# Moving the products of the forget and decay sums three slab pairs back, with their tables in a tile of their own

## The chip, the cores and the metric

The kernel runs on one core of a Trainium2 chip. The metric is the device time of one execution in microseconds (us); several executions are measured, and their median is given.

## What is computed

One layer of a decoder with two token mixers that read the same normalized input `h` (1024 tokens by 1024 channels): a state-space branch (SSD) and an attention branch with forget gates. Cut to what the change touches:

```python
proj = h @ w_in                       # slabs z, xbc, dt, q, k, v, z_att, f, gates
dt = softplus(dt_raw + dt_bias)       # 16 heads
a = dt * -exp(a_log)
a_cs = cumsum(a within chunks of 128 tokens)
lmat = exp(a_cs[l] - a_cs[s])         # decay inside a chunk; exp(a_cs) also carries the states
log_f = log_sigmoid(f_logit + b_f)    # 8 heads
f_cum = cumsum(log_f over all 1024 tokens)
logits = q k^T * scale + f_cum[q] - f_cum[k]
```

Both sums along tokens are made by matrix products: a lower triangle of ones sums within a block of 128 tokens, and a matrix of ones adds what lies in earlier blocks.

## The kernel before

The matrix products run in float32 as three products of a high and a low half (`hh` and `hl` for the input, `wh` and `wl` or `sh` and `sl` for the weights). The work has these stages: the normalized input and its halves; a first slab of v with the columns of `dt` and `f`; then 19 pairs of weight slabs of 128 columns (`PAIRS`, counted here from 0); then the SSD stage mixed with the rest of v and some of q and k; attention; and the output products.

A pair (`c_pair`, from line 463) is computed by a scheme with seven products instead of eight: VectorE makes sums and differences of the four raw weight tiles (lines 481 to 484), ScalarE rounds each of the seven forms to its high half and GpSimd makes the low half (`split`, lines 102 and 103), TensorE does seven products of 12 matmuls each over tiles of 128 by 512 (lines 499 to 501: high by high, high by low, low by high), and VectorE adds the products up in PSUM (lines 508 to 521). The forms are named `f1`, `f6`, `f7`, `f5`, `f4`, `f2`, `f3` in this order. The products go into eight PSUM buffers, three of the pool `mm` and five of the pool `pp`; a product can start only when its buffer's earlier product has been taken out.

What takes a product out depends on the slab. A gate slab has a tanh on ScalarE (line 188). A slab for the convolution is copied to `xp` (line 538), and when both halves are there VectorE makes four passes of 128 by 1024 and a last product (lines 542, 545 and 548, with a tanh on ScalarE between, line 547). A slab for z has a tanh on ScalarE (line 528) and a product on VectorE that reads the PSUM buffer (line 529, into `zt`). Pairs 0 and 2 are gates, pairs 1, 3 and 5 are convolutions, pair 4 is z. In front of some pairs the kernel also makes sums of the later stages' weights (`w_sums`, lines 583 to 598: loads, two sums on VectorE at 590 and 591, two on GpSimd, stores).

The softplus chain `dt_chain` (lines 366 to 402) is called in front of pair 2. It loads 24 columns for 1024 tokens from `d_scr` into the tile `tmp` (line 622), computes the softplus by a series on VectorE (lines 372 to 385, one exponential on ScalarE), negates the forget part into a table `lf` of 64 columns (line 390), makes the running sums over blocks `pre` in another 64 (line 394), and multiplies both by `tri` and `ones` on TensorE (lines 396 and 397). The result is copied (line 399) and stored to `f_scr` (line 400), which the attention stage reads. `tmp` is one of four buffers of the pool `ev` that also holds the slabs on their way out, so its tables last only as long as it is held. `ssm_sums` (lines 404 to 430), called in front of pair 3, does the same for the decay: `a` from `dt` (line 407), three products (412 to 414), and copies and exponentials into `acs`, `dec`, `ed`, `a_scr` and `e_scr`, which the SSD stage reads.

The order on each engine is not that of the code: a scheduler places the instructions ahead of time by an estimate, engine by engine, and on the chip each engine then executes its list strictly in order. A list's instruction that waits holds up all that stand behind it on the same engine. The DMAs are all issued by SyncE (SP), also in order.

Of the kernel before, what the change touches and what calls it, by code (L numbers as in the profile page):

```python
# [24 lines left out]
F32 = mybir.dt.float32  # L25
# [6 lines left out]
P = 128  # L32
# [37 lines left out]
def build(ctx, tc, t):  # L70
    nc = tc.nc
    V, A, G, PE, SP = nc.vector, nc.scalar, nc.gpsimd, nc.tensor, nc.sync

    const = ctx.enter_context(tc.tile_pool(name="const", bufs=1))
# [8 lines left out]
    def ev(name):  # L83
        return evp.tile([P, 1028], F32, tag="ev", bufs=4, name=name)
# [63 lines left out]
    ones = const.tile([P, P], F32, name="ones")  # L148
    V.memset(ones, 1.0)
    tri = const.tile([P, P], F32, name="tri")  # L150
# [9 lines left out]
    f_scr = dram.tile([64, P], F32, name="f_scr")  # L160
# [170 lines left out]
    dt = const.tile([P, NC, SH], F32, name="dt")  # L331
    acs = const.tile([P, NC, SH], F32, name="acs")
    dec = const.tile([P, NC, SH], F32, name="dec")
    ed = const.tile([P, NC, 8], F32, name="ed")

    def gate_slab(j):
        evac, store = gate_out(j)
        c_slab(t["w_c"], G0 + j, hh, hl, evac)
        store()
# [23 lines left out]
    with tc.tile_pool(name="pa", bufs=1, side="right") as pa, \  # L363
            tc.tile_pool(name="pap", bufs=1, space=PSUM) as pap:

        def dt_chain(dtf, tmp):

            def sl(i):
                return tmp[:, i * 192:(i + 1) * 192].rearrange("p (c n) -> p c n", n=24)
            b3 = hb[:, 0:24].rearrange("p (o n) -> p o n", o=1).broadcast_to([P, 8, 24])  # L370
            v, e, s, p = dtf, sl(1), sl(2), sl(3)
            V.tensor_tensor(out=v, in0=v, in1=b3, op=ALU.add)
            V.tensor_scalar(out=v[:, :, 16:24], in0=v[:, :, 16:24], scalar1=-1.0, scalar2=None, op0=ALU.mult)
            V.scalar_tensor_tensor(out=e, in0=v, scalar=-1.0, in1=v, op0=ALU.mult, op1=ALU.max)
            A.activation(out=e, in_=e, func=AF.Exp, scale=-1.0)
            V.tensor_scalar(out=s, in0=e, scalar1=2.0, scalar2=None, op0=ALU.add)
            V.reciprocal(out=s, in_=s)
            V.tensor_tensor(out=s, in0=s, in1=e, op=ALU.mult)
            V.tensor_tensor(out=e, in0=s, in1=s, op=ALU.mult)
            V.tensor_scalar(out=p, in0=e, scalar1=1.0 / 15, scalar2=None, op0=ALU.mult)  # L380
            for n in (13, 11, 9, 7, 5, 3):
                V.scalar_tensor_tensor(out=p, in0=p, scalar=1.0 / n, in1=e, op0=ALU.add, op1=ALU.mult)
            V.scalar_tensor_tensor(out=p, in0=p, scalar=1.0, in1=s, op0=ALU.add, op1=ALU.mult)
            V.tensor_scalar(out=v, in0=v, scalar1=0.0, scalar2=None, op0=ALU.max)
            V.scalar_tensor_tensor(out=v, in0=p, scalar=2.0, in1=v, op0=ALU.mult, op1=ALU.add)


            lf = tmp[:, 192:256].rearrange("p (h c) -> p h c", h=8)
            pre = tmp[:, 256:320].rearrange("p (h c) -> p h c", h=8)
            V.tensor_scalar(out=lf, in0=v[:, :, 16:24].rearrange("p c h -> p h c"), scalar1=-1.0, scalar2=None,  # L390
                            op0=ALU.mult)
            V.memset(pre[:, :, 0:1], 0.0)
            for c in range(1, 8):
                V.tensor_tensor(out=pre[:, :, c:c + 1], in0=pre[:, :, c - 1:c], in1=lf[:, :, c - 1:c], op=ALU.add)
            ps = pap.tile([P, 512], F32, tag="pp", bufs=5, name="pp")
            PE.matmul(ps[0:64, 0:P], lhsT=tmp[:, 192:256], rhs=tri, start=True, stop=False)
            PE.matmul(ps[0:64, 0:P], lhsT=tmp[:, 256:320], rhs=ones, start=False, stop=True)
            ft = tmp[0:64, 320:320 + P]
            V.tensor_copy(out=ft, in_=ps[0:64, 0:P])
            SP.dma_start(out=f_scr, in_=ft)  # L400

            V.tensor_copy(out=dt, in_=v[:, :, 0:16])

        def ssm_sums():
            a = ev("a")
# [205 lines left out]
        tmp = ev("tmp")  # L611
# [7 lines left out]
        for n, (sa, sb) in enumerate(PAIRS):  # L619
            if n == 2:  # L620
                tmp = ev("tmp")
                SP.dma_start(out=tmp[:, 0:192], in_=d_scr)
                dt_chain(tmp[:, 0:192].rearrange("p (c n) -> p c n", n=24), tmp)
            if n == 3:
                ssm_sums()
            for wn, p in WPREP.get(n, ()):
                if wn == "g":
                    gb = out_gate(gb, p)
                elif wn == "G":
                    gb = gate_sum(gb)  # L630
                else:
                    w_sums(wn, p, gb if wn == "o" else None)
            (ea, fa), (eb, fb) = slab_out(sa), slab_out(sb)
            c_pair(sa, sb, ea, eb)
            fa()
            fb()


    with tc.tile_pool(name="sd", bufs=1, side="right") as sd, \
# [152 lines left out]
        for tb in range(8):  # L792
            PE.matmul(rps[:, 2 * tb:2 * tb + 1], lhsT=sacc[:, tb * P:(tb + 1) * P], rhs=ones[:, 0:1],
                      start=True, stop=True)
        rc = const.tile([P, 8], F32, name="rc")
        V.tensor_scalar(out=rc, in0=rps[:, 0:16].rearrange("p (a two) -> p a two", two=2)[:, :, 0],
                        scalar1=1.0 / 1024, scalar2=4 * EPS, op0=ALU.mult, op1=ALU.add)
        G.tensor_tensor(out=rc, in0=rc, in1=mhalf, op=ALU.pow)
# [287 lines left out]
    with tc.tile_pool(name="finp", bufs=1, space=PSUM) as fpp_:  # L1086
# [73 lines left out]
        for i in OOUT:  # L1160
# [7 lines left out]
            if i != OOUT[-1]:  # L1168
                ps = [bank() for _ in range(4)]
# [6 lines left out]
            else:  # L1176
                fs = [w_in("o", i, k) for k in range(4)]
                for tb in range(4):
                    ps = bank()
# [70 lines left out]
```

## Time and profile before

| | us |
|---|---|
| median of 3 runs | 1305.86 |
| lowest and highest | 1300.53, 1307.06 |
| the profiled execution | 1302.24 |
| its span, first to last instruction | 1300.5 |
| TensorE busy | 1182.4 |
| VectorE busy | 934.5 |
| GpSimd busy | 759.7 |
| ScalarE busy | 594.6 |

The profile is of one execution. In a timeline each row has the start, the duration, the engine (PE is TensorE, DVE is VectorE, ACT is ScalarE, POOL is GpSimd, SP is SyncE), the line, the instruction with its output and inputs, how many were merged (x), and in brackets how long the engine had been idle and what it waited for. Matmuls overlap: a row of 0.39 us is followed by the next after 0.23. Lists of groups give the count, the busy time, the mean of one in ns, and the idle time before.

### The profile page before, as it was taken

How to read it: one execution, taken by the hardware profiler on the slowest of the kernel's cores; microseconds unless marked ns; L12 is line 12 of the kernel's file. 1: busy time of each engine (PE TensorE's matmuls, PEld its weight loads, DVE VectorE, ACT ScalarE, POOL GpSimd, SP SyncE). 2: the span in 40 equal slices, each digit the busy share in tenths (PEclk: the TensorE clock that was granted, in tenths of full speed). 3: DMA queues.
4: the chain of work that ended last, by engine and by line, in shares of the span. 5: the costliest groups of instructions: out<-in, count | busy, mean ns of one | idle time of the engine just before them, and what ended most of it. 6: DMA issues, size and time to landing. Idle time of an engine off the chain costs nothing. (4 is left out here: it accounts for less than half of the span.)

```text
span 1300.5 us, 18848 instructions
## 1 busy us (share of the span) xinstructions
PE 1182.4 (91%) x6206; PEld 988.6 (76%) x6206; DVE 934.5 (72%) x1610; ACT 594.6 (46%) x1194; POOL 759.7 (58%) x636
## 2 busy tenths in 40 slices
PE   4889929998998899999988999999999998999896
PEld 3678817876876688799878888888887786888685
DVE  6855474976799576546779873555566978999997
ACT  5453313323233233377667743445456453354354
POOL 3226543556666466627878876445446645687666
PEclk9899969999998899999999999999999999999998
DMA  8664541345438375655646648633227518666234
GB/s 343 236 220 137 181 148 63 127 153 175 173 85 301 121 256 186 226 196 157 213 153 186 192 155 294 224 112 99 91 99 232 189 66 304 219 197 196 56 114 145
DMA packets 109022, 228.29 MB, mean 176 GB/s; under 512 B 12362, under 2 KB 20220, under 8 KB 107900
## 3 DMA queue, kind: packets, MB, share of 16 engines
q1 hardware_dynamic: 108924, 227.09, 52.4%
q8 instruction: 49, 0.80, 0.2%
q14 instruction: 49, 0.40, 0.1%
HBM read 159.14 MB, written 67.90 MB: 175 GB/s over the span
## 5 line engine op out<-in xcount | busy, mean ns | idle before, releaser
L103 POOL TENSOR_TENSOR wl<-wr,wh 128x512 fp32r<-128x512 f32 (+1 forms) x188 | 280.2, 1502 | 166.6 <-ACT wh L102 149.8
L102 ACT CAST wh<-wr 128x512 fp32r<-128x512 f32 (+1 forms) x214 | 129.3, 618 | 177.8 <-DMA wr<-w_c 64.7
L103 POOL TENSOR_TENSOR sl<-sr,sh 128x512 fp32r<-128x512 f32 x57 | 91.1, 1605 | 87.4 <-ACT sh L102 74.6
L116 PE MATMUL mm<-hl,wh 128*128 128x512 f32 x288 | 116.8, 405 | 1.8 <-DVE hl L310 1.8
L115 PE MATMUL mm<-hh,wh 128*128 128x512 f32 x288 | 115.8, 407 | 0.4 <-DVE ql L972 0.4
L117 PE MATMUL mm<-hh,wl 128*128 128x512 f32 x288 | 116.1, 404 | 0.0
L140 PE MATMUL mm<-wh,hh 128*128 128x256 f32 (+1 forms) x256 | 74.3, 292 | 4.9 <-DVE tmp L351 4.9
L102 ACT CAST sh<-sr 128x512 fp32r<-128x512 f32 x57 | 33.8, 617 | 93.5 <-DVE sr L482 74.3
L141 PE MATMUL mm<-wl,hh 128*128 128x256 f32 (+1 forms) x256 | 74.5, 292 | 0.0
L142 PE MATMUL mm<-wh,hl 128*128 128x256 f32 (+1 forms) x256 | 74.4, 292 | 0.0
L1027 ACT ACTIVATE pr<-pr,sm 128x1024 f32<-128x1024 f32 (+3 forms) x64 | 49.9, 780 | 51.5 <-DVE sm L1026 42.1
L1030 POOL TENSOR_SCALAR pr<-pr,sm 128x1024 f32<-128x1024 f32 (+3 forms) x64 | 48.8, 765 | 36.0 <-DVE sm L1029 29.3
L1022 DVE CUSTOM_DVE_ANT_0 pr<-lg,fb 128x512 f32<-128x512 f32 (+1 forms) x96 | 51.6, 551 | 21.5 <-PE lg L1021 13.1
L116 PEld LDWEIGHTS mm<-hl,wh 128*128 128x128 f32 x288 | 55.4, 192 | 13.4 <-DVE hl L310 2.6
L117 PEld LDWEIGHTS mm<-hh,wl 128*128 128x128 f32 x288 | 55.3, 192 | 10.9
L1013 POOL TENSOR_SCALAR_AFFINE_SELECT fb<-fb 128x128 f32<-128x128 f32 x64 | 21.0, 330 | 71.9 <-DVE sm L1022 58.0
L1046 DVE TENSOR_TENSOR ptl<-tp,pth 128x512 fp32r<-128x512 f32 (+1 forms) x80 | 50.1, 632 | 17.9 <-ACT pth L1045 17.6
L115 PEld LDWEIGHTS mm<-hh,wh 128*128 128x128 f32 x288 | 54.8, 193 | 10.4 <-DVE ql L972 0.6
L1045 ACT CAST pth<-tp 128x512 fp32r<-128x512 f32 (+1 forms) x80 | 42.4, 543 | 40.5 <-PE tp L1042 31.3
L692 ACT ACTIVATE ab<-ab,acs 128x128 f32<-128x128 f32 x128 | 41.0, 391 | 32.2 <-DMA ab<-a_scr 30.5
L140 PEld LDWEIGHTS mm<-wh,hh 128*128 128x128 f32 x256 | 49.1, 193 | 5.3 <-DVE tmp L351 5.1
L141 PEld LDWEIGHTS mm<-wl,hh 128*128 128x128 f32 x256 | 49.4, 193 | 0.2
(401 smaller groups left out, 3923.5 us busy)
## 6 DMA issues: line engine op xcount, KB each, us to landing
wr<-w_c SPq DMA_DIRECT2D x116, 256.0 KB, 3.5
wa<-w_ada SPq DMA_DIRECT2D x8, 1024.0 KB, 11.3
g_scr<-gt SPq DMA_DIRECT2D x16, 512.0 KB, 4.1
ab<-a_scr SPq DMA_DIRECT2D x32, 256.0 KB, 3.6
gt<-g_scr SPq DMA_DIRECT2D x32, 256.0 KB, 3.2
wr<-w_ps SPq DMA_DIRECT2D x28, 256.0 KB, 2.9
wr<-w_pa SPq DMA_DIRECT2D x28, 256.0 KB, 3.1
wr<-so SPq DMA_DIRECT2D x28, 256.0 KB, 2.7
```

The lines of the kernel that those rows point to most:

```text
L102: A.copy(out=hi[:, :n], in_=raw[:, :n])
L103: eng.tensor_tensor(out=lo[:, :n], in0=raw[:, :n], in1=f32(hi[:, :n]), op=ALU.subtract)
L115: PE.matmul(ps, lhsT=hi[:, cs], rhs=xh[k][:, hs], start=(k == 0), stop=False)
L116: PE.matmul(ps, lhsT=hi[:, cs], rhs=xl[k][:, hs], start=False, stop=False)
L117: PE.matmul(ps, lhsT=lo[:, cs], rhs=xh[k][:, hs], start=False, stop=(k == 7))
L140: PE.matmul(o, lhsT=xh[k][:, ts], rhs=hi[:, cs], start=(k == 0), stop=False)
L141: PE.matmul(o, lhsT=xh[k][:, ts], rhs=lo[:, cs], start=False, stop=False)
L142: PE.matmul(o, lhsT=xl[k][:, ts], rhs=hi[:, cs], start=False, stop=(k == 7))
L1022: V.tensor_tensor_reduce(out=pr[:, n0:n1], in0=lg[:, :n1 - n0], in1=fb[:, n0:n1], op0=ALU.add, op1=ALU.min, scale=1.0, scalar=BIG, accum_o ...
L1027: A.activation(out=pr[:, :n], in_=pr[:, :n], func=AF.Exp, scale=-1.0, bias=sm[:, 0:1], accum_out=sm[:, 1:2])
L1030: G.tensor_scalar(out=pr[:, :n], in0=pr[:, :n], scalar1=sm[:, 1:2], scalar2=0.5, op0=ALU.mult, op1=ALU.mult)
L1046: V.tensor_tensor(out=ptl[:, :w], in0=tp[:, :w], in1=f32(pth[:, :w]), op=ALU.subtract)
```

## The change

`dt_chain` now writes `lf` and `pre` into a new constant tile `fl` (128 by 128), so that they last when `tmp` is given back, and ends with the copy to `dt`. The two products, the copy and the store of the forget sums become `f_sums`; the copy goes back into `fl`. `f_sums` and `ssm_sums` are both called in front of pair 5, instead of in front of pair 2 (inside the chain) and pair 3. At the end of the SSD stage the tile `rc` of 8 columns takes the first columns of `fl` instead of a tile of its own. Line numbers behind the new tile are one or two higher.

```diff
--- before.py
+++ after.py
@@ -332,6 +332,7 @@
     acs = const.tile([P, NC, SH], F32, name="acs")
     dec = const.tile([P, NC, SH], F32, name="dec")
     ed = const.tile([P, NC, 8], F32, name="ed")
+    fl = const.tile([P, P], F32, name="fl")
 
     def gate_slab(j):
         evac, store = gate_out(j)
@@ -385,21 +386,21 @@
             V.scalar_tensor_tensor(out=v, in0=p, scalar=2.0, in1=v, op0=ALU.mult, op1=ALU.add)
 
 
-            lf = tmp[:, 192:256].rearrange("p (h c) -> p h c", h=8)
-            pre = tmp[:, 256:320].rearrange("p (h c) -> p h c", h=8)
+            lf = fl[:, 0:64].rearrange("p (h c) -> p h c", h=8)
+            pre = fl[:, 64:128].rearrange("p (h c) -> p h c", h=8)
             V.tensor_scalar(out=lf, in0=v[:, :, 16:24].rearrange("p c h -> p h c"), scalar1=-1.0, scalar2=None,
                             op0=ALU.mult)
             V.memset(pre[:, :, 0:1], 0.0)
             for c in range(1, 8):
                 V.tensor_tensor(out=pre[:, :, c:c + 1], in0=pre[:, :, c - 1:c], in1=lf[:, :, c - 1:c], op=ALU.add)
+            V.tensor_copy(out=dt, in_=v[:, :, 0:16])
+
+        def f_sums():
             ps = pap.tile([P, 512], F32, tag="pp", bufs=5, name="pp")
-            PE.matmul(ps[0:64, 0:P], lhsT=tmp[:, 192:256], rhs=tri, start=True, stop=False)
-            PE.matmul(ps[0:64, 0:P], lhsT=tmp[:, 256:320], rhs=ones, start=False, stop=True)
-            ft = tmp[0:64, 320:320 + P]
-            V.tensor_copy(out=ft, in_=ps[0:64, 0:P])
-            SP.dma_start(out=f_scr, in_=ft)
-
-            V.tensor_copy(out=dt, in_=v[:, :, 0:16])
+            PE.matmul(ps[0:64, 0:P], lhsT=fl[:, 0:64], rhs=tri, start=True, stop=False)
+            PE.matmul(ps[0:64, 0:P], lhsT=fl[:, 64:128], rhs=ones, start=False, stop=True)
+            V.tensor_copy(out=fl[0:64], in_=ps[0:64, 0:P])
+            SP.dma_start(out=f_scr, in_=fl[0:64])
 
         def ssm_sums():
             a = ev("a")
@@ -621,7 +622,8 @@
                 tmp = ev("tmp")
                 SP.dma_start(out=tmp[:, 0:192], in_=d_scr)
                 dt_chain(tmp[:, 0:192].rearrange("p (c n) -> p c n", n=24), tmp)
-            if n == 3:
+            if n == 5:
+                f_sums()
                 ssm_sums()
             for wn, p in WPREP.get(n, ()):
                 if wn == "g":
@@ -792,7 +794,7 @@
         for tb in range(8):
             PE.matmul(rps[:, 2 * tb:2 * tb + 1], lhsT=sacc[:, tb * P:(tb + 1) * P], rhs=ones[:, 0:1],
                       start=True, stop=True)
-        rc = const.tile([P, 8], F32, name="rc")
+        rc = fl[:, 0:8]
         V.tensor_scalar(out=rc, in0=rps[:, 0:16].rearrange("p (a two) -> p a two", two=2)[:, :, 0],
                         scalar1=1.0 / 1024, scalar2=4 * EPS, op0=ALU.mult, op1=ALU.add)
         G.tensor_tensor(out=rc, in0=rc, in1=mhalf, op=ALU.pow)
```

On TensorE, in before, between the product of pair 2 with the form `f4` (into the buffer mm_1754) and the one with `f1` (into pp_1696); `tmp` and `tri` are the tables named above:

```order
L501 MATMUL mm_1754<-thb2_1204,wl_1681 128x512
L499 MATMUL mm_1754<-thb3_1228,wh_1680 128x512
L500 MATMUL mm_1754<-tlb3_1229,wh_1680 128x512
L501 MATMUL mm_1754<-thb3_1228,wl_1681 128x512
L396 MATMUL pp_1622<-tri_76,tmp_1593 64x128
L499 MATMUL pp_1696<-hh0_240,wh_1664 128x512
L500 MATMUL pp_1696<-hl0_248,wh_1664 128x512
L501 MATMUL pp_1696<-hh0_240,wl_1665 128x512
```

In the changed kernel, TensorE's list behind the same product with `f4` (now mm_1750) has the one with `f2` (pp_1765, on `hh4` to `hh7`); those with `f1` and `f6` have moved ahead of those with `f7`, `f5` and `f4`, and no product of the sums is in pair 2:

```order
L502 MATMUL mm_1750<-thb2_1205,wl_1677 128x512
L500 MATMUL mm_1750<-thb3_1229,wh_1676 128x512
L501 MATMUL mm_1750<-tlb3_1230,wh_1676 128x512
L502 MATMUL mm_1750<-thb3_1229,wl_1677 128x512
L500 MATMUL pp_1765<-hh4_244,wh_1680 128x512
L501 MATMUL pp_1765<-hl4_252,wh_1680 128x512
L502 MATMUL pp_1765<-hh4_244,wl_1681 128x512
L500 MATMUL pp_1765<-hh5_245,wh_1680 128x512
```

So the matmul of line 396 has left this place, and the order of the seven products within pair 2 is now that of the code.

On TensorE, in before, at the end of pair 4: the last matmuls of its product with `f3` (mm_2147), and behind them the first product of pair 5 (pp_2216, `f1`):

```order
L501 MATMUL mm_2147<-hh6_246,sl_2049 128x512
L499 MATMUL mm_2147<-hh7_247,sh_2048 128x512
L500 MATMUL mm_2147<-hl7_255,sh_2048 128x512
L501 MATMUL mm_2147<-hh7_247,sl_2049 128x512
L499 MATMUL pp_2216<-hh0_240,wh_2184 128x512
L500 MATMUL pp_2216<-hl0_248,wh_2184 128x512
L501 MATMUL pp_2216<-hh0_240,wl_2185 128x512
L499 MATMUL pp_2216<-hh1_241,wh_2184 128x512
```

The same place in the changed kernel: behind the product with `f3` (mm_2126) stand the two products of the forget sums (lines 400 and 401), and behind those pair 5's product with `f2` (mm_2290), which in before stood sixth in its pair:

```order
L500 MATMUL mm_2126<-hh7_247,sh_2027 128x512
L501 MATMUL mm_2126<-hl7_255,sh_2027 128x512
L502 MATMUL mm_2126<-hh7_247,sl_2028 128x512
L400 MATMUL pp_2144<-tri_76,fl_836 64x128
L401 MATMUL pp_2144<-ones_74,fl_836 64x128
L500 MATMUL mm_2290<-hh4_244,wh_2205 128x512
L501 MATMUL mm_2290<-hl4_252,wh_2205 128x512
L502 MATMUL mm_2290<-hh4_244,wl_2206 128x512
L500 MATMUL mm_2290<-hh5_245,wh_2205 128x512
```

The sums have come to this place, and the product into an `mm` buffer has moved ahead of `f1`; the decay sums' three products follow it.

On VectorE, in before, the end of pair 3's convolution (cv_1999), the weight sums (sr_2344) and pair 4's products for z (zt_2008, zt_2007; mm_2115 holds the product with `f4`):

```order
L548 SCALAR_TENSOR_TENSOR cv_1999<-xp_1839,cv_1999 128x1024
L591 TENSOR_TENSOR sr_2344<-sr_2343,wr_2335 128x512
L529 SCALAR_TENSOR_TENSOR zt_2008<-zt_2008,pp_2098 128x512
L518 TENSOR_TENSOR mm_2131<-mm_2131,pe_2052 128x512
L529 SCALAR_TENSOR_TENSOR zt_2008<-zt_2008,mm_2115 128x512
L521 TENSOR_TENSOR mm_2147<-mm_2147,pe_2055 128x512
L535 MEMSET xp_2165 128x3
L529 SCALAR_TENSOR_TENSOR zt_2007<-zt_2007,mm_2131 128x512
L529 SCALAR_TENSOR_TENSOR zt_2007<-zt_2007,mm_2147 128x512
```

The same place in the changed kernel (cv_1978, sr_2345, zt_1987, zt_1986; mm_2094 holds the product with `f4`):

```order
L549 SCALAR_TENSOR_TENSOR cv_1978<-xp_1818,cv_1978 128x1024
L592 TENSOR_TENSOR sr_2345<-sr_2344,wr_2336 128x512
L530 SCALAR_TENSOR_TENSOR zt_1987<-zt_1987,pp_2077 128x512
L519 TENSOR_TENSOR mm_2110<-mm_2110,pe_2031 128x512
L530 SCALAR_TENSOR_TENSOR zt_1987<-zt_1987,mm_2094 128x512
L522 TENSOR_TENSOR mm_2126<-mm_2126,pe_2034 128x512
L408 SCALAR_TENSOR_TENSOR a_2149<-dt_832,hb_81 128x128
L402 COPY fl_836<-pp_2144 64x128
L530 SCALAR_TENSOR_TENSOR zt_1986<-zt_1986,mm_2110 128x512
L530 SCALAR_TENSOR_TENSOR zt_1986<-zt_1986,mm_2126 128x512
```

The start of the decay sums (a_2149) and the copy of the forget sums (fl_836) now stand between pair 4's products for z, behind the one that reads mm_2094.

## The prediction

> **What bounds the kernel now.** I read the page first, slice by slice, to see which engine is full in the stage that is edited; then the list of waits of TensorE, then its timeline around the longest wait, then VectorE's timeline in the same stretch, since VectorE is named as releaser. On the page the share of each engine comes first, then the 40 slices of 32.5 us:
>
> ```profile
> PE 1182.4 (91%) x6206; PEld 988.6 (76%) x6206; DVE 934.5 (72%) x1610; ACT 594.6 (46%) x1194; POOL 759.7 (58%) x636
> PE   4889929998998899999988999999999998999896
> PEclk9899969999998899999999999999999999999998
> ```
>
> TensorE is busy for 91% of the span and is the bound nearly everywhere; only slice 6 (162 to 195 us) is nearly empty, and the granted clock falls there too. The waits of TensorE between 120 and 320 us, and its timeline on both sides of the longest (start, duration, instruction, idle time before it):
>
> ```profile
> PE pp L396 <- DVE tmp L390: 26.3, 1, 26.3
> ...
> 162.35 0.39 PE L499 MATMUL mm<-tha,wh 128*128 128x512 f32 x1
> ...
> 170.42 0.40 PE L501 MATMUL mm<-thb,wl 128*128 128x512 f32 x1
> 197.16 0.69 PE L396 MATMUL pp<-tri,tmp 128*64 128x128 f32 x2 [26.34 <-DVE tmp L390]
> 197.78 0.80 PE L499 MATMUL pp<-hh,wh 128*128 128x512 f32 x1
> ...
> 201.62 0.39 PE L499 MATMUL pp<-hh,wh 128*128 128x512 f32 x1
> ```
>
> The product of the forget sums (line 396) stands in TensorE's queue ahead of the first products of slab pair 2 (pairs are counted from 0), and it waited 26.34 us for the softplus chain. Nine matmuls behind it took 197.78 to 201.62, 3.84 us, where the pace before was 0.233 apart (2.1 us): the stop cost 1.7 us more. VectorE in that time:
>
> ```profile
> 169.69 2.49 DVE L542 TENSOR_SCALAR cv<-xp,cols 128x1024 f32<-128x1024 f32 x2
> ...
> 186.92 0.67 DVE L372 TENSOR_TENSOR tmp<-tmp,hb 128x192 f32<-128x192 f32 x1 [1.89 <-DMA tmp<-d_scr]
> ...
> 196.87 0.23 DVE L390 TENSOR_SCALAR tmp<-tmp 128x64 f32<-128x64 f32 x1
> ...
> 204.97 0.28 DVE L399 COPY tmp<-pp 64x128 f32<-64x128 f32 x1 [6.39 <-PE pp L397]
> ...
> 257.95 0.67 DVE L529 SCALAR_TENSOR_TENSOR zt<-zt,mm 128x512 f32<-128x512 f32 x1
> ```
>
> VectorE did the convolution of pair 1 from 169.69 on, then the chain to 197.1. So it was at work while TensorE stood still, and it stood still 6.39 us itself for the second product (line 397). TensorE's stop was VectorE's chance to work off its queue: that is what the change takes away from it.
>
> **The removed wait.** With the two sum products gone from this place, the next in TensorE's queue are the products of pair 2, from 162.35 on. Their forms were there. GpSimd, which makes the low half of each form last, for pair 2 (and the start of its work for pair 3):
>
> ```profile
> 155.38 1.29 POOL L103 TENSOR_TENSOR wl<-wr,wh 128x512 fp32r<-128x512 f32 x1 [4.25 <-ACT wh L102]
> 158.86 3.02 POOL L103 TENSOR_TENSOR sl<-sr,sh 128x512 fp32r<-128x512 f32 x2 [2.19 <-ACT sh L102]
> ...
> 165.61 1.29 POOL L103 TENSOR_TENSOR sl<-sr,sh 128x512 fp32r<-128x512 f32 x1
> ...
> 182.63 3.52 POOL L103 TENSOR_TENSOR sl<-sr,sh 128x512 fp32r<-128x512 f32 x1 [9.34 <-ACT sh L102]
> ```
>
> The first form of pair 2 is ready at 156.7, the next two at 161.9, and the last, whose product is the seventh, at 166.9. Then GpSimd is idle for the better part of the 9.34 us ahead of 182.63. How long a pair takes is read from the first matmuls of pairs 4, 5 and 6:
>
> ```profile
> 231.35 0.39 PE L499 MATMUL pp<-hh,wh 128*128 128x512 f32 x1
> ...
> 250.77 0.39 PE L499 MATMUL pp<-hh,wh 128*128 128x512 f32 x1
> ...
> 270.19 0.39 PE L499 MATMUL mm<-hh,wh 128*128 128x512 f32 x1
> ```
>
> 19.42 us each. Pairs 2, 3 and 4 without a stop end at 162.35 + 3 x 19.42 = 220.6. There the two forget products now stand (0.7 us for both, an estimate from the 0.62 that the first took in the slow restart), and TensorE is free at 221.3 for pair 5. In before pair 5 began at 250.77, so on TensorE alone the lead is 29.5 us. The three products of the decay sums also move to this place, out of pair 3; in before they took 215.38 to 215.96, 0.6 us, which leaves 28.9:
>
> ```profile
> 215.38 0.38 PE L412 MATMUL pp<-a,tri 128*128 128x128 f32 x2
> ...
> 215.96 0.48 PE L499 MATMUL pp<-hh,wh 128*128 128x512 f32 x1
> ```
>
> **The wait that takes its place.** The order of the changed kernel puts a product of pair 5 (its sixth, with the form `f2` on `hh4` to `hh7`, into an `mm` buffer) right behind the forget products, ahead of pair 5's first. Its buffer is the one that VectorE frees when it has finished the silu product of pair 4 (`zt_1987<-zt_1987,mm_2094`, line 529 in before, 530 now). In before that instruction ran at 257.95, 7.2 us after TensorE was through with pair 4, and nobody waited, because the matching product stood later. Now everything on TensorE stands behind it. So the question is when VectorE gets there. One row gives all its work from the start of pair 1's convolution to the end of that instruction; a second gives the part of the decay sums that writes from or into `a` (five instructions), which now stands behind it:
>
> ```profile
> 169.69:258.62 88.93, 62.59 (x266) 49.96 (x265) 65.63 (x94) 25.76 (x43) 37.51 (x24) 0.85 0.32 105
> ...
> 204.00:219.00 15.00, 1.21 (x5) 1.00 0.32 114
> ...
> 216.24 0.29 DVE L416 COPY acs<-pp 128x128 f32<-128x128 f32 x1 [1.33 <-PE pp L414]
> ```
>
> The columns of the first row are busy time and count of TensorE, its weight loads, VectorE, ScalarE and GpSimd. VectorE was busy 65.63 of 88.93 us; the rest, 23.3 us, was waiting, nearly all a consequence of TensorE's stop. Taking off 1.21, 0.29 (line 416) and 0.28 (line 399) leaves 63.85 us that must still be done in order, so VectorE cannot get there before 169.69 + 63.85 = 233.5. TensorE is there at 221.3: a wait of at least 12.2 us replaces the one of 26.3.
>
> The work may also take longer, because GpSimd's instructions now lie in 64 us instead of 89. The same VectorE instructions show two durations:
>
> ```profile
> 178.49 2.47 DVE L545 SCALAR_TENSOR_TENSOR cv<-xp,cols,cv 128x1024 f32<-128x1024 f32 x2
> 181.48 0.68 DVE L483 TENSOR_TENSOR wr<-wr 128x512 f32<-128x512 f32 x1
> ...
> 232.18 1.78 DVE L483 TENSOR_TENSOR wr<-wr 128x512 f32<-128x512 f32 x1
> 237.67 5.74 DVE L545 SCALAR_TENSOR_TENSOR cv<-xp,cols,cv 128x1024 f32<-128x1024 f32 x3
> ...
> L545 DVE SCALAR_TENSOR_TENSOR cv<-xp,cols,cv 128x1024 f32<-128x1024 f32 x12 | 18.3, 1566 | 0.0
> L591 DVE TENSOR_TENSOR sr<-sr,wr 128x512 f32<-128x512 f32 x2 | 3.2, 1615 | 0.0
> L483 DVE TENSOR_TENSOR wr<-wr 128x512 f32<-128x512 f32 x3 | 3.1, 1048 | 0.0
> ```
>
> With GpSimd idle (ahead of 182.63) they take 1.24 and 0.68, later up to 1.91 and 1.78. By the three groups, which are those of this window, the excess was 12 x 0.33 + 2 x 0.93 + 3 x 0.37 = 7.0 us, with GpSimd busy 37.51 of 88.93 us (42%). The same work in 64 us is 59%, 1.4 times as dense: 2.8 us more if the excess follows the density. Bounds: -2.0 (GpSimd runs dry while TensorE stands, and the three passes at 237.67 are as quick as those at 178.49) and 7.0 (the excess doubles). I take 2.8, by the density, so 236.3.
>
> The Trainium skill ("SBUF — State Buffer", Who interferes with whom) speaks against the change here: an elementwise instruction of VectorE with both inputs in SBUF and a GpSimd instruction reading SBUF exclude each other for the whole of the instruction that came first. The rows agree in kind (1.78 against 0.68); what it would make of the time if every pass met is the third rival.
>
> **The sum.** Pair 5 then takes 19.42 and the decay products 0.6; after a stop of 15 us I count the slow restart again, 1.7. Pair 6 begins at 236.3 + 20.0 + 1.7 = 258.0 instead of 270.19: 12.2 us gained. Behind it, TensorE waited in before at these places:
>
> ```profile
> 273.75 0.50 PE L499 MATMUL pp<-thb,sh 128*128 128x512 f32 x1 [0.63 <-ACT sh L102]
> 274.79 0.50 PE L499 MATMUL pp<-tha,wh 128*128 128x512 f32 x1 [0.31 <-ACT wh L102]
> 298.48 0.50 PE L501 MATMUL pp<-tha,wl 128*128 128x512 f32 x1 [1.16 <-POOL wl L103]
> 304.61 0.50 PE L499 MATMUL pp<-thb,wh 128*128 128x512 f32 x1 [0.78 <-DVE zt L529]
> ...
> 397.57 0.79 PE L499 MATMUL mm<-thb,wh 128*128 128x512 f32 x1 [6.46 <-ACT gt L188]
> 434.23 0.80 PE L499 MATMUL mm<-tha,sh 128*128 128x512 f32 x1 [5.40 <-DVE zt L529]
> ```
>
> All hang on VectorE and its helpers, which have gained 22.3 us (257.95 + 0.67 to 236.3) where TensorE gained 12.2, so I let the first four go: 2.9 us. The last two belong to the output gate's sums, 130 us later; I leave them. Gain 12.2 + 2.9 = 15.1 us. What else moves costs nothing: in SyncE's queue the stores of the forget and decay sums go behind the loads of the next weight sums instead of those of pair 4, and are first read in the attention and SSD stages, long after the slab pairs; the copy to `dt` only comes earlier; the memset of `fl` goes to the program's start, where VectorE waits for inputs; `rc` in `fl` is written after the SSD stage, when the sums have long been stored. Pair 3's second form: ahead of its sum VectorE now has eight convolution passes and four short instructions, 8 x 1.24 + 4 x 0.68 = 12.6, so 182.3, and a cast and 1.29 of GpSimd later it is there, at about 184.2, against 162.35 + 19.42 + 2.8 = 184.6. Some us late would cost nothing, since TensorE would only wait the less at pair 5; without that wait they would count in full. Should VectorE be over 10 us late already at the forget sums' input, TensorE stops there and not one product later, with the same end.
>
> The profiled execution took 1302.24 us, 1300.5 of it span; it becomes 1287.1. It lay 3.6 us under the median of the runs, 1305.86, so I forecast 1290.8 for the median. Own range: at best the silu product ends at 231.5, there is no slow restart, and besides the four waits one of the last two goes (5.4): 270.19 - 251.5 + 2.9 + 5.4 = 27.0; at worst it ends at 240.5 and nothing is regained: 270.19 - 262.2 = 8.0. That is 1279 to 1298.
>
> **The rivals.** First, the whole gain: VectorE keeps up and no new wait arises; 28.9 us, 1277. It would have to do 63.85 us of work in 51.6; even without any excess it is 56.9. Against it stands the sum above; for it, only that part of the excess came from the stop. 8%.
>
> Second, the gain is lost behind: the change reorders VectorE's and SyncE's rows up to the last pairs, and each row put ahead of one whose input comes a product later can hold the in-order queues by up to a product, 19.42 / 7 = 2.8 us. Three or four such places take 8 to 11 of the 15: 1299 to 1302. For it: VectorE has the two later waits of 6.46 and 5.40 on its account. Against: its queue is ahead by more than TensorE's. 16%.
>
> Third, slower: VectorE and GpSimd exclude each other through the whole stretch. Without excess VectorE needs 63.85 - 7.0 = 56.9; the 24 GpSimd instructions of the window at 1.29 each are 31.0; one after the other 87.9 us, which puts the silu product at 257.6, pair 6 at 257.6 + 21.7 = 279.3, 9.1 later than before: 1315. It turns to a loss when the silu product ends after 270.19 - 21.7 = 248.5. Against it: the window already shows 37.51 us of GpSimd beside 65.63 of VectorE. 6%.
>
> **How the numbers follow.** Forecast 70%, rivals 8, 16 and 6. A measurement of this kernel tells about 0.5%, 6.5 us, from no change. Faster by more than that: nearly all of the forecast's cases, the first rival and a quarter of the second, 0.81; within it the rest of the second and the forecast's lower end, 0.14; slower 0.05. The range reaches to the first rival below and to the second's upper end: 1277 to 1302.
>
> **What would show it.** In the profile of the changed kernel: no wait at 170 us; pair 2 following at 162.35; the forget products near 221; right behind them one wait of 12 to 18 us, put down to VectorE's silu product of `zt`, ending between 233 and 240; VectorE without long gaps from 170 to there; pair 6 starting near 258. The forecast is wrong if TensorE passes that place without a stop, if the wait is longer than 27 us, or if the lead at pair 6 isn't the lead at 480 us give or take 4.

## The result, and the profile after

| | before | after |
|---|---|---|
| median of 5 runs each | 1302.2 | 1293.1 |
| lowest and highest | 1300.53, 1307.06 | 1291.91, 1296.01 |
| the profiled execution | 1302.24 | 1295.8 |
| its span | 1300.5 | 1294.1 |

The changed kernel takes 0.9928 of the time of the kernel before (95% interval 0.9899 to 0.9956): 9.1 us less. Two more runs of the kernel before took its median from the 1305.86 of the prediction to 1302.2, about what its profiled execution had. The forecast was 1290.8, with a gain of 15.1 us. The time is only 2.3 us off, but the gain is 6 us smaller: the kernel before came out 3.7 us faster than it was taken to be.

First the page of the changed kernel, the busy times, TensorE's 40 slices and the granted clock (slices of 32.35 us):

```profile
PE 1182.6 (91%) x6206; PEld 991.6 (77%) x6206; DVE 943.3 (73%) x1610; ACT 594.3 (46%) x1194; POOL 757.9 (59%) x636
...
PE   4789999499889899999998999999999998999896
...
PEclk9899999699999899999999999999999899999999
```

The slice that had a 2 now has a 9; two slices later there is a 4, and the clock falls there. The stop has moved by about 47 us (197.16 to 244.60) and become shorter. TensorE's timeline of the changed kernel shows it: the first matmuls of pairs 0, 2, 3 and 4, the forget products, what stands behind them, and the first matmul of pair 6:

```profile
126.61 0.40 PE L500 MATMUL mm<-hh,wh 128*128 128x512 f32 x1
...
165.34 0.40 PE L500 MATMUL pp<-hh,wh 128*128 128x512 f32 x1
...
184.69 0.39 PE L500 MATMUL pp<-hh,wh 128*128 128x512 f32 x1
...
206.82 0.39 PE L500 MATMUL pp<-hh,wh 128*128 128x512 f32 x1
...
226.53 0.38 PE L401 MATMUL pp<-ones,fl 128*64 128x128 f32 x2
244.60 0.80 PE L500 MATMUL mm<-hh,wh 128*128 128x512 f32 x1 [17.69 <-DVE zt L530]
...
267.30 0.40 PE L500 MATMUL mm<-hh,wh 128*128 128x512 f32 x1
```

Pair 2 follows pair 1 without a stop. At 226.53 the forget products are through, and the next product, `f2` of pair 5, waits 17.69 us for VectorE's silu product. The profiled execution was 2.99 us late at pair 2 already (165.34 against 162.35), at places that the change doesn't touch; below I take these 2.99 us off. VectorE in the changed kernel, from the convolution of pair 1 to the silu product:

```profile
171.28 0.69 DVE L591 TENSOR_TENSOR sr<-wr 128x512 f32<-128x512 f32 x1 [5.47 <-DMA wr<-w_ps]
...
173.88 2.51 DVE L543 TENSOR_SCALAR cv<-xp,cols 128x1024 f32<-128x1024 f32 x2
...
198.51 1.24 DVE L385 TENSOR_SCALAR tmp<-tmp 128x192 f32<-128x192 f32 x1
...
216.34 1.33 DVE L396 COPY dt<-tmp 128x128 f32<-128x128 f32 x1
...
221.96 2.53 DVE L543 TENSOR_SCALAR cv<-xp,cols 128x1024 f32<-128x1024 f32 x2
224.41 6.72 DVE L546 SCALAR_TENSOR_TENSOR cv<-xp,cols,cv 128x1024 f32<-128x1024 f32 x3
...
243.87 0.67 DVE L530 SCALAR_TENSOR_TENSOR zt<-zt,mm 128x512 f32<-128x512 f32 x1
```

In the kernel before, two of the chain's instructions had been far shorter (there lines 384 and 402):

```profile
189.19 0.26 DVE L384 TENSOR_SCALAR tmp<-tmp 128x192 f32<-128x192 f32 x1
...
197.02 0.22 DVE L402 COPY dt<-tmp 128x128 f32<-128x128 f32 x1
```

The window of that stretch in the changed kernel (columns as in the prediction):

```profile
173.88:244.54 70.66, 51.07 (x220) 40.39 (x218) 70.12 (x86) 23.30 (x39) 39.35 (x24) 0.90 0.39 125
```

VectorE was busy for 70.12 of 70.66 us: there is no gap, it was behind all the way. GpSimd was busy for 39.35 us, 56% of the stretch.

### The profile page after: what moved, and what is told of

Same layout as the page of the kernel before. It is cut to its first block, busy times and chain, and to the rows that moved or that the text cites. A ratio compares the mean times of both kernels' runs of the same rounds, so it can differ in the third digit from the quotient of the medians.

```text
span 1294.1 us, 18844 instructions
## 1 busy us (share of the span) xinstructions
PE 1182.6 (91%) x6206; PEld 991.6 (77%) x6206; DVE 943.3 (73%) x1610; ACT 594.3 (46%) x1194; POOL 757.9 (59%) x636
## 5 line engine op out<-in xcount | busy, mean ns | idle before, releaser
L546 DVE SCALAR_TENSOR_TENSOR cv<-xp,cols,cv 128x1024 f32<-128x1024 f32 x30 | 50.4, 1701 | 0.0
```

Source lines behind the costliest of these rows:

```text
L546: V.scalar_tensor_tensor(out=v, in0=xp[:, i:i + S], scalar=cols[:, R_CW + 10 * i + j:R_CW + 10 * i + j + 1], in1=v, op0=ALU.mult, op1=ALU.add)
```

## The experiments

The theory: the removed stop had been VectorE's pause; now VectorE is behind, its work is drawn out beside GpSimd's, and TensorE is stopped by the first product that needs VectorE. The rivals are named with each run. The medians are of 4 to 12 runs, each against 11 to 17 of the kernel before on the same chip (5 against 5 in the first row). The kernel before had medians from 1302.2 to 1303.92 in these series, so rows are compared by their ratios, and rows whose intervals overlap are not told apart by the time. "Pair 6" is its first matmul counted from that of pair 0 (146.80 in the kernel before: 270.19 less 123.39).

| run | median | ratio (95%) | pair 6 |
|---|---|---|---|
| changed kernel | 1293.1 | 0.9928 (0.9899 to 0.9956) | 140.69 |
| forget products alone | 1292.78 | 0.9912 (0.9893 to 0.9931) | 137.59 |
| decay products alone | 1310.69 | 1.0055 (1.0039 to 1.007) | 154.57 |
| both at pair 7 | 1292.71 | 0.992 (0.9903 to 0.9937) | 128.96 |
| low halves on ScalarE | 1275.82 | 0.9795 (0.9773 to 0.9818) | 122.68 |
| chain at pair 0 | 1288.85 | 0.9903 (0.9879 to 0.9928) | 134.11 |
| both at pair 7, `a` early | 1290.4 | 0.9912 (0.9886 to 0.9938) | 129.09 |
| kernel before, chain at pair 0 | 1284.73 | 0.987 (0.9842 to 0.9898) | 131.05 |
| chain at pair 0, `a` early | 1285.55 | 0.9869 (0.9844 to 0.9894) | 124.46 |
| `a` early | 1293.05 | 0.992 (0.9899 to 0.9941) | 133.01 |
| chain at pair 0, `a` early, pairs 3 and 4 swapped | 1281.35 | 0.9828 (0.9804 to 0.9851) | 120.77 |
| chain at pair 0, `a` early, sums at pair 2 | 1284.96 | 0.9859 (0.9832 to 0.9887) | 125.15 |
| output weight sums earlier | 1301.44 | 0.9986 (0.9967 to 1.0004) | 139.42 |

**The forget products alone.**

```diff
+            if n == 3:
+                ssm_sums()
             if n == 5:
                 f_sums()
-                ssm_sums()
```

> One part alone: the forget products are called in front of pair 5, the decay products stay in front of pair 3. In its order the decay products stand behind three products of pair 3, with the other four products of pair 3 behind them, and pair 5's products keep their order. The theory (TensorE is held by VectorE's backlog; where it stands in the list decides how much): the stop at pair 2 is gone, and one of 10 to 20 us comes at the decay products, since VectorE has `dt` ready only at about 205 to 212 us and TensorE is there at about 193; behind it no stop over 5 us up to pair 6, which begins between 262 and 270 (270.19 in the kernel before); median 1288 to 1298. The rival (the gain of the change comes from the forget part, and the sixth product's place eats it): no stop over 5 us at the decay products, pair 6 before 255, median under 1285.

1292.78. The decay products stopped TensorE for 9.37 us, after two waits of 2.16 and 2.33 us for forms of pair 3; pair 6 began at 261.47. The stop and pair 6 lie half a us under what was expected, all else as the theory had it: the stop goes to where the next input from VectorE is needed.

**The decay products alone.**

```diff
+            if n == 2:
+                f_sums()
             if n == 5:
-                f_sums()
                 ssm_sums()
```

> The other part alone: the decay products are called in front of pair 5, the forget products stay in front of pair 2, out of the new tile. In its order pair 5's product with `f2` stands first in its pair, as in the changed kernel, and the forget products stop TensorE at pair 2, as in the kernel before. The theory (a product that stands ahead costs what VectorE is behind at that place): the stop of about 26 us at pair 2 stays, and since VectorE's silu product ended 7.9 us behind TensorE's pair 4 in the kernel before (258.62 against 250.77), a wait of 5 to 8 us comes at pair 5's `f2`; pair 6 begins 4 to 8 us later than in the kernel before, part of which comes back at the later waits; median 1302 to 1309. The rival (the order in pair 5 costs nothing where VectorE has had its pause): no wait over 3 us there, median 1299 to 1303.

1310.69, slower than the kernel before. Its two stops:

```profile
198.04 0.69 PE L400 MATMUL pp<-tri,fl 128*64 128x128 f32 x2 [26.96 <-DVE fl L391]
...
256.83 0.80 PE L500 MATMUL mm<-hh,wh 128*128 128x512 f32 x1 [6.14 <-DVE zt L530]
```

A product that stands ahead of its pair costs what VectorE is behind there, even after VectorE's pause: 6.14 us, as the theory had it. The time is 1.7 us over its upper end; pair 6 is 7.8 us later than in the kernel before, and little came back.

**Both sums in front of pair 7.**

```diff
-            if n == 5:
+            if n == 7:
```

> Both sums are called in front of pair 7 instead of pair 5; pairs 2 to 6 keep the order of products that they have without sums, and pair 7's two `mm` products that go ahead are its first two. The theory (VectorE is 17.7 us behind when TensorE comes to pair 5; what this costs is decided by the place of the product that needs VectorE): with pair 5's products in their order that product stands 5 products (13.9 us) later, so the stop of 17.7 us goes and waits of 3 to 8 us in all come in its place between 226 and 290 us, for the buffers that VectorE takes out; median 1280 to 1288. The rival (VectorE's work up to there is the bound, whatever the order): stops of 13 to 18 us in all in the same stretch, spread over pairs 4 to 6, median 1290 to 1296.

1292.71, the rival's time. Between pairs 4 and 6 the theory nearly held (5.55 us at pair 5's `f4`, 1.56, 0.65, 0.73 and 0.31 behind it, 8.8 in all), and pair 6 began 11.7 us earlier than in the changed kernel. Then came a stop that neither had:

```profile
291.32 0.80 PE L413 MATMUL pp<-a,tri 128*128 128x128 f32 x2 [10.69 <-DVE xp L536]
```

VectorE in this run finished `a` at 291.27; the row names another instruction, but this is the input:

```profile
290.25 1.02 DVE L408 SCALAR_TENSOR_TENSOR a<-dt,hb 128x128 f32<-128x128 f32 x1
```

**GpSimd's load taken off** (shortened; `n` is the pair):

```diff
-                eng.tensor_tensor(out=lo, in0=raw, in1=f32(hi), op=ALU.subtract)
+                if n in (3, 4, 5):
+                    A.copy(out=lo, in_=raw)
+                else:
+                    G.tensor_tensor(out=lo, in0=raw, in1=f32(hi), op=ALU.subtract)
```

> The changed kernel with GpSimd's load taken off the stretch: in pairs 3, 4 and 5 the low halves of the 21 forms are plain copies on ScalarE of what was to be split; the subtraction of the high halves is left out. TensorE's list is the same. The theory (VectorE came to the silu product late because its instructions were drawn out beside GpSimd's; uncontended, the work between the convolution of pair 1 and that product is 63.85 - 7.0 = 56.9 us against 70.7 in the changed kernel): VectorE needs 56 to 60 us for it, the wait at pair 5's `f2` falls from 17.7 to 3 to 7 us, median 1279 to 1287. The rival (VectorE's time there is its own: instructions at their usual length, and waits for other engines): 66 us or more, the wait over 13 us, median 1290 to 1295.

1275.82, below what the theory gave, and the wait at `f2` fell to 3.48 us. The window from the convolution of pair 1 to the end of the silu product, then the end of its chain and two passes of pair 3's convolution:

```profile
169.91:224.29 54.38, 50.97 (x223) 41.21 (x221) 52.28 (x86) 32.99 (x59) 6.27 (x3) 1.00 0.49 159
```

```profile
203.88 0.23 DVE L391 TENSOR_SCALAR fl<-tmp 128x64 f32<-128x64 f32 x1
204.02 0.22 DVE L396 COPY dt<-tmp 128x128 f32<-128x128 f32 x1
...
208.30 2.48 DVE L554 SCALAR_TENSOR_TENSOR cv<-xp,cols,cv 128x1024 f32<-128x1024 f32 x2
```

The same 86 instructions took 54.4 us where the changed kernel took 70.7. The copy to `dt` is back at 0.22 from 1.33, a pass at 1.24 from 2.2. So the 16 us that VectorE needed more are GpSimd's work beside it; the rival falls. This kernel leaves the subtraction out, so it doesn't compute the layer, and ScalarE has 21 more copies: the lengths of VectorE's instructions are the evidence, and 1275.82 us is not a time that the whole computation reached.

**The chain in front of pair 0.**

```diff
-            if n == 2:
+            if n == 0:
                 tmp = ev("tmp")
```

> The changed kernel with the softplus chain called in front of pair 0 instead of pair 2; both sums stay in front of pair 5 and TensorE's list is that of the changed kernel, product for product. In the changed kernel's trace the chain's instructions took 17.3 us of VectorE between 195.5 and 221 us; between 120 and 165 us VectorE was busy for only some 16 of 45 us. The theory (VectorE's backlog sets the end of the wait, and the chain beside GpSimd is its largest part): the silu product of pair 4 ends 15 to 18 us earlier, TensorE waits at pair 5's `f2` at most 4 us instead of 17.7, pair 6 begins between 242 and 249 us, median 1273 to 1281. The rival (the two engines' conflict moves on to the convolution passes, so that VectorE comes as late): the wait stays over 8 us, median 1285 to 1293.

1288.85, with a wait of 10.72 us at `f2`: the rival's numbers. Pair 6 began 6.6 us earlier than in the changed kernel; the intervals of the two times overlap. My theory had the weights wrong: the chain is 7.0 of the 17.69 us, not most of it. VectorE in this run:

```profile
206.34 1.34 DVE L482 TENSOR_TENSOR sr<-wr 128x512 f32<-128x512 f32 x1 [4.22 <-DMA wr<-w_c]
...
212.25 2.53 DVE L543 TENSOR_SCALAR cv<-xp,cols 128x1024 f32<-128x1024 f32 x2 [0.47 <-ACT xp L539]
214.70 6.79 DVE L546 SCALAR_TENSOR_TENSOR cv<-xp,cols,cv 128x1024 f32<-128x1024 f32 x3
...
234.23 0.67 DVE L530 SCALAR_TENSOR_TENSOR zt<-zt,mm 128x512 f32<-128x512 f32 x1
```

VectorE has gaps now: it isn't behind, it waits for a load and for pair 3's last half. But pair 3's convolution stands ahead of the silu product in its list and took from 212.25 on, 22.65 us to that product's end (17.44 with the low halves on ScalarE, by 206.85 and 224.29). That is a second reason for the wait, which the backlog had covered.

**Both sums in front of pair 7, `a` early** (`dec` is free until the sums' end; shortened: the shapes are left out, and the lines that made `a` in `ssm_sums` go):

```diff
+    af = dec.rearrange("p c h -> p (c h)")
...
             V.tensor_copy(out=dt, in_=v[:, :, 0:16])
+            A.activation(out=hb[:, 24:40], in_=hb[:, 24:40], func=AF.Exp)
+            V.scalar_tensor_tensor(out=af, in0=dt, scalar=-1.0, in1=hb[:, 24:40], op0=ALU.mult, op1=ALU.mult)
```

> Both sums in front of pair 7 as in the run before (1292.7), but `a`, the input of the decay products, is made at the end of the softplus chain and lies in the tile `dec` until the products have read it; so the decay products wait for a buffer only. In the run before, TensorE came to pair 6 at 252 us, some 12 us ahead of the changed kernel, and then stood 10.69 us at the decay products of pair 7, whose `a` stands in VectorE's list behind the convolution of pair 5. The theory (a product that is put ahead of its pair waits for whatever VectorE has in front of its input, and this took the gain back): no stop over 5 us between 270 and 330 us, median 1280 to 1285. The rival (VectorE's backlog is there whatever its list's order, and stops TensorE at the next product that needs it): stops of 8 us or more in all between 270 and 330 us, median 1289 to 1294.

1290.4: the stop of 10.69 us is gone, but 4.62 us came at pair 7's third product, whose buffer waits for VectorE's copy of the forget sums. The stop was the theory's, the time the rival's: pair 6 is 11.6 us ahead of the changed kernel, the median only 2.7, which the intervals don't tell from nothing.

**The kernel before with the chain in front of pair 0** (the diff of the chain at pair 0, in the kernel before).

> The kernel before with one number changed: the softplus chain with its forget products is called in front of pair 0 instead of pair 2; the decay products stay in front of pair 3. In its order the forget products stand behind the third product of pair 0, the second of them behind the sixth. The theory (what cost 26 us was the chain's place behind the convolution of pair 1 on VectorE, not the products' place on TensorE): no stop over 5 us for the chain at pair 0, where VectorE has time, and the decay products in pair 3 wait 2 to 9 us for `a`; median 1276 to 1288, below the changed kernel. The rival (the products must stand far behind the chain): stops of over 12 us in all at the two places, median 1292 or more.

1284.73, below the changed kernel, with the forget products right behind the chain and the decay products in front of pair 3, as before. The stops:

```profile
138.11 0.69 PE L396 MATMUL pp<-tri,tmp 128*64 128x128 f32 x2 [5.81 <-DVE tmp L390]
...
200.41 0.49 PE L412 MATMUL pp<-a,tri 128*128 128x128 f32 x2 [1.96 <-DVE a L407]
```

The first is 0.8 us over what I gave it, the second just under. What cost 26 us was the chain's place on VectorE.

**The chain in front of pair 0 and `a` early, sums at pair 5.**

> The changed kernel with the softplus chain in front of pair 0 and `a` made at its end, in `dec`; the sums stay in front of pair 5. Pair 5's products then keep their order, with the five products of the sums ahead of them. The theory: nothing that stands ahead needs VectorE, so there is no stop over 3 us between 160 and 330 us; pairs 2 to 5 follow each other at 19.42 us, and pair 6 begins at 162.4 + 4 x 19.42 + 1.3 = 241.4, up to 244; median 1271 to 1278. The rival (VectorE's work up to there is still the bound): stops of 5 us or more in that stretch, median 1280 to 1288.

1285.55, the rival's time, with the theory's short stops (2.41 us the longest, at pair 5; 1.41 and 0.64 in pair 3). But pair 6 came 4 us later than the latest expected (248.76, pair 2 at 163.04): pair 3 took 4.1 us more than 19.42, twice its two waits (last section), and pair 5 2.7 us more. Behind pair 6 waits of 2.24, 2.44, 4.59 and 6.18 us for VectorE and its helpers remained.

**`a` early, nothing else.**

> The changed kernel with `a` made at the end of the softplus chain, in `dec`; chain in front of pair 2 and sums in front of pair 5 as in the changed kernel. In its order all five products of the sums stand in front of pair 5 and pair 5's products keep their order; `f2` is sixth again. VectorE has the work of the changed kernel. Theory A (the place of `f2` costs the wait): the 17.7 us go, waits of under 8 us in all up to pair 6, median 1280 to 1287. Theory B (VectorE is late, and TensorE, whose eight buffers hold about one pair, is stopped by the next buffers in whatever order): TensorE stops 8 to 14 us at pair 5's third or fourth product, which take the buffers of pair 4's last products and of the forget sums; what it is ahead at pair 6 it loses at pairs 6 and 7; median 1288 to 1293. After the runs with the sums in front of pair 7 (1292.7 and 1290.4) I hold B.

1293.05, the changed kernel's time. TensorE waited 4.19 and 4.39 us in pair 5 in place of 17.69 at `f2`:

```profile
228.25 0.79 PE L500 MATMUL pp<-hh,wh 128*128 128x512 f32 x1 [4.19 <-DVE pe L509]
...
239.85 0.80 PE L500 MATMUL pp<-tha,wh 128*128 128x512 f32 x1 [4.39 <-DVE zt L530]
```

Pair 6 began 7.7 us earlier, and nothing of it was left in the median. The place of `f2` set the form of the stop, and VectorE the time: theory B, with stops of 8.6 us in all, though the first of them came at pair 5's first product already.

**Pairs 3 and 4 swapped**, on the kernel with the chain at pair 0 and `a` early:

```diff
-(XB0, XB0 + 1), (Z0, Z0 + 1), (XB0 + 2, XB0 + 3),
+(Z0, Z0 + 1), (XB0, XB0 + 1), (XB0 + 2, XB0 + 3),
```

> The run with the chain in front of pair 0 and `a` early (1285.55), with pairs 3 and 4 swapped: pair 3 is now the one for z and pair 4 a convolution. So the silu products of z no longer stand behind a convolution on VectorE, and the buffers of the pair ahead of the sums are freed by ScalarE's copies; two convolutions follow each other, in pairs 4 and 5. The theory (a convolution on VectorE just ahead of instructions that free buffers is what is left of the waits): the 2.4 us wait at pair 5 and the 2.2 us wait at pair 7 go, pair 6 begins 2 to 3 us earlier, median 1281 to 1284. The rival (two convolutions in a row fill VectorE: 20 passes of 1.2 to 2 us in 39 us beside the rest): new stops of 5 us or more in pairs 6 and 7, median 1286 to 1293.

1281.35, by the median the fastest kernel with the whole computation: faster than the kernel before by 1.7%. Its interval overlaps those of the three kernels at 1284.73 to 1285.55. Between pairs 2 and 6 no wait is over 0.9 us. The wait at pair 7 stayed, against the theory (4.11 us), and two later ones, 4.59 and 6.18 us without the swap, grew:

```profile
280.89 0.80 PE L500 MATMUL pp<-thb,wh 128*128 128x512 f32 x1 [4.11 <-DVE zt L530]
371.15 0.79 PE L500 MATMUL mm<-thb,wh 128*128 128x512 f32 x1 [9.54 <-ACT gt L188]
411.31 0.79 PE L500 MATMUL mm<-tha,sh 128*128 128x512 f32 x1 [9.43 <-DVE zt L530]
```

**The sums back in front of pair 2**, chain at pair 0 and `a` early:

> The run with the chain in front of pair 0 and `a` early (1285.55), with both sums back in front of pair 2, so that their products are not put off. The theory (once the chain lies where VectorE has time, the products need not be moved behind anything): no stop for the sums, pairs 2 to 5 at 19.4 to 20.5 us each, median 1283 to 1288. The rival (the products need the distance to the chain, or the copies and exponentials of the sums, now between the convolutions of pairs 1 and 3, hold VectorE up): stops of 4 us or more between 160 and 245 us that this run's parent does not have, median over 1289.

1284.96, the time of the sums at pair 5, as the theory had it. The theory gave no stop for the sums; one of 5.41 us came at pair 3, for ScalarE's exponential that frees the decay sums' buffer, as the rival had it. So with the chain out of the way these two places cost the same in the time; other places were not tried.

**The output weight sums one pair earlier.** In the changed kernel the lead over the kernel before falls by 3.3 us at these rows:

```profile
531.18 0.50 PE L500 MATMUL mm<-thb,sh 128*128 128x512 f32 x1 [2.17 <-ACT sh L102]
...
532.87 0.50 PE L502 MATMUL mm<-thb,sl 128*128 128x512 f32 x1 [0.96 <-POOL sl L103]
```

```diff
-15: [('o', 0)], 16: [('o', 1)], 17: [('o', 2)], 18: [('o', 3)]
+14: [('o', 0)], 15: [('o', 1)], 16: [('o', 2)], 17: [('o', 3)]
```

> The changed kernel with the four sums of the output weights made one pair earlier (in front of pairs 14 to 17 instead of 15 to 18); nothing changes up to pair 12. In the changed kernel the lead over the kernel before falls from 9.2 to 5.9 us at 531 us, in pair 18, where TensorE waits 2.17 and 0.96 us for a form; the loads of that pair's weights were issued only 6.1 us earlier than in the kernel before, behind loads and stores of these sums. The theory (this piece of the gain is given back at a place that is bound by the loads into the four `wr` buffers): without the sums in front of pair 18 the two waits go and the lead stays above 8 us to 580 us, median 1288 to 1291. The rival (the loads come as late for another reason, or the sums bring the same wait to pair 17): median 1292 to 1295.

1301.44, slower than the changed kernel: the wait stayed (2.49 us) and another of 2.79 us came two pairs earlier. TensorE was 14.0 us ahead of the kernel before at 451.82 and 1.1 us at 544.47. The theory falls here; why the lead shrinks in pair 18 stays open.

## Why the prediction was right, and where it was off

- **The wait that takes the place of the old one** came where it was forecast, for the instruction that was forecast, and 17.69 us long (12 to 18).
- **When VectorE gets there** is the term that was mis-sized. Forecast 236.3, measured 244.54 - 2.99 = 241.6. Of these 5.2 us (before rounding), 1.2 are a later start (173.88 - 2.99 = 170.9 instead of 169.69, behind a load), and 4.0 are the excess beside GpSimd: 70.66 us instead of 63.85 + 2.8. Scaling the excess of the kernel before by GpSimd's density missed that the chain had run there while GpSimd was almost idle, busy for 1.79 of 10.28 us in this window of the kernel before (VectorE 9.35):

```profile
186.92:197.20 10.28, 0.04 (x1) 0.04 (x1) 9.35 (x23) 0.36 (x1) 1.79 (x2) 0.50 0.23 71
```

  All but the first two of the chain's short instructions had met nobody there, and so showed no excess. In the changed kernel the excess is 6.8 us (70.66 less 63.85), just inside the upper bound of 7.0. TensorE came 2.6 us late too, at 226.91 - 2.99 = 223.9 instead of 221.3, since pair 3's forms came late: 15.0 + 5.2 - 2.6 = 17.6, beside 17.69 measured.
- **Pair 6** was to begin at 258.0 and began at 267.30 - 2.99 = 264.3: 5.2 from VectorE, 1.1 from a slower restart of pair 5 (22.8 us from the silu product to pair 6, forecast 21.7). The gain there is 5.9 us instead of 12.2.
- **The waits behind it** gave back more than the 2.9 us of the sum. By the row at 388.19 the lead was 12.4 us:

```profile
388.19 0.79 PE L500 MATMUL mm<-thb,wh 128*128 128x512 f32 x1 [6.31 <-ACT gt L188]
425.69 0.80 PE L500 MATMUL mm<-tha,sh 128*128 128x512 f32 x1 [6.17 <-DVE zt L530]
```

  (397.57 - 388.19 + 2.99.) I had left out two waits of the kernel before, of which the first went too and the second fell from 0.97 to 0.62 us (at 310.25):

```profile
317.90 0.50 PE L499 MATMUL mm<-thb,sh 128*128 128x512 f32 x1 [1.89 <-ACT sh L102]
319.60 0.50 PE L501 MATMUL mm<-thb,sl 128*128 128x512 f32 x1 [0.97 <-POOL sl L103]
```

  The last two waits of the forecast's list (now at 388.19 and 425.69) were to stay as they were; the second grew by 0.8.
- **The end.** 12.4 - 0.8 - 3.3 in pair 18 and small amounts make 1300.5 - 1294.1 + 2.99 = 9.4, beside 9.1 by the medians. The forecast's own test, that the lead at pair 6 be that at 480 us give or take 4, failed: 5.9 and 12.0. That the total fell into the range is in part luck: a loss ahead of pair 6 and a gain behind it, neither of which the sum had, partly cancelled, and so the step of the sum that carries the lead from pair 6 to the end unchanged but for 2.9 us is wrong.
- **The rivals.** The whole gain didn't come. Loss behind came in one place, 3.3 us. Full exclusion of VectorE and GpSimd didn't come, but the mechanism decided the size: with GpSimd's subtractions away the wait is 3.48 us.
- **Who is late** was right only in part. Besides the backlog there is pair 3's convolution ahead of the silu product. The chain accounts for 7.0 us of the wait (17.69 to 10.72 with the chain at pair 0), GpSimd's low halves for 14.2 (to 3.48), and the two overlap.

## What to carry to other kernels

A stop of the bound engine can be the pause in which its helper catches up: take the stop away, and it comes back at the next place that needs the helper, so before moving the product ask where the helper has time. Here calling the softplus chain two pairs earlier, in a stretch where VectorE was busy for 16 of 45 us, gained twice what putting its products off did, 17.6 us against 9.1. A lead at one place isn't a gain at the end: in three runs leads of 14 to 18 us at pair 6 ended as 11 to 12, while in the two that only move the chain to pair 0 leads of 12.7 and 15.8 became 13.5 and 17.6.

## What the runs showed of the hardware that I had not expected

Short instructions of VectorE with a single input in SBUF are drawn out beside GpSimd too, and by the largest factor: the copy to `dt` of 128 by 128 took 0.22 us alone and 1.33 beside GpSimd's subtractions, a tensor-scalar of 128 by 192 took 0.26 and 1.24. I had reckoned with instructions of two SBUF inputs. The Trainium skill ("SBUF — State Buffer", Who interferes with whom) names copies and tensor-scalar instructions in their two-port modes among those that take the shared ports; the rows agree that these two are slowed, though no run shows their mode. They show the price: 1.0 to 1.1 us a meeting, somewhat less than a GpSimd subtraction (1.29 us), for these as for a pass of 128 by 1024 (1.24 to 2.2).

A short stop of TensorE can cost about as much again behind it. In the run with the chain at pair 0 and `a` early, the waits of 1.41 and 0.64 us in pair 3 (at 186.74 and 188.11) were followed by matmuls 0.43 us apart instead of 0.23, while the granted clock was 0.87:

```profile
189.06 0.63 PE L502 MATMUL pp<-thb,sl 128*128 128x512 f32 x1
...
191.62 0.63 PE L502 MATMUL pp<-thb,sl 128*128 128x512 f32 x1
```

```profile
190.00:198.00 8.00, 8.00 (x32) 6.46 (x31) 5.27 (x8) 3.16 (x6) 7.99 (x6) 0.87 0.92 324
```

There are six steps between the two matmul rows; in the window's row the granted clock is the third number from the end. Pair 3 took 23.55 us in that run (182.39 to 205.94), 4.1 over the undisturbed 19.42, for waits of 2.05. The Trainium skill ("TensorE: Matmul & The Clock Gate", What's actually happening) gives half rate after at least one idle window of about 3.4 us; here two waits of 2.05 us in all, with some matmuls between them, were enough.

The length alone doesn't decide it. In the same run a longer wait, in pair 5, cost next to nothing more:

```profile
234.80 0.50 PE L500 MATMUL pp<-tha,wh 128*128 128x512 f32 x1 [2.41 <-DVE zt L530]
...
237.68 0.40 PE L500 MATMUL pp<-tha,sh 128*128 128x512 f32 x1
```

The twelve steps between these rows are 0.24 us each, and behind the 0.44, 0.62 and 0.89 us that the changed kernel waits in its pair 3 the matmuls were 0.23 apart. What decides it, no run here shows.
